# Layer 0's feed-forward: 14 of its 22 pairs of up tiles as seven block products in place of eight

## The chip, the cores and the metric

The kernel runs on one core of a Trainium2 chip. TensorE (PE) multiplies, VectorE (DVE) and ScalarE (ACT) do the elementwise work, GpSimd (POOL) a little of it, SyncE (SP) starts the transfers. Each engine works through its own list of instructions in the order written, and waits on semaphores for the others. The metric is the device time of one execution, in microseconds (us): the median of three runs of the kernel before is 1257.51, from 1257.15 to 1257.99.

## The reference

Two networks run one after the other on 256 tokens of width 1024. The first is one layer of gated linear attention with its feed-forward. The second has two layers and two streams: 256 latent tokens (the first network's output) and 256 context tokens. Layer 0 is neighbourhood attention, layer 1 grouped-query attention. Both streams are normalised, scaled and shifted by rows of an adaptive modulation that is computed from a conditioning vector. The stage that matters here is layer 0's feed-forward:

```python
def swiglu_ffn(h, w_in, w_out):
    a, g = jnp.split(h @ w_in, 2, axis=-1)
    return (jax.nn.silu(a) * g) @ w_out
...
        mod_l = (silu_c @ ada_w[i] + ada_b[i])[:, None, :]
        mod_c = (silu_cc @ ada_w[i] + ada_b[i])[None, None, :]
...
        h = h + g2_l * swiglu_ffn(ada_norm(h, norm_ffn[i], sh2_l, sc2_l), ffn_w_in[i], ffn_w_out[i])
        if ctx_out:
            hc = hc + g1_c * y_c
            hc = hc + g2_c * swiglu_ffn(ada_norm(hc, norm_ffn[i], sh2_c, sc2_c), ffn_w_in[i], ffn_w_out[i])
```

The width is 1024, the hidden width 2816: 22 tiles of 128 for `a` and 22 for `g`. A tile of `a` and the tile of `g` that is multiplied with it are called a pair. Layer 0 computes both streams, layer 1 only the latents' result.

## The kernel before

**Products.** Every 32-bit product is made of three matmuls (`mm3`, lines 192 to 195): each operand `x` is held as `h`, a rounded copy that PE multiplies fast, and `l = x - h`, and `h h + l h + h l` is summed in PSUM. So every weight that arrives has to be split first: ACT writes `h` (line 178), DVE subtracts (line 179). A weight unit is 128 x 1024 numbers (512 KB); `UNITS` lists all of them in the order of use, `wnext` hands out the next one, starts loads four ahead into five `raw` buffers, and splits ahead by a small number (`cap`).

**The feed-forward of layer 0.** Its tokens, 256 latents and 256 context tokens, lie transposed, split and side by side in `fT`, so a matmul moves 512 columns. It runs in two parts of 11 pairs. In the ups (`ffn_up`) each of the pair's two units is multiplied, 8 blocks of 128 times three matmuls, into a PSUM bank of 512; then `ffn_act` makes silu (ACT, line 1111), the product of the two banks (DVE, line 1112) and its split (lines 1118 and 1119). Behind a part's ups its down (`ffn_down0`) multiplies the 11 hidden tiles into four token tiles, one 512-wide half of the output at a time, and `gated` (lines 1080 and 1081) scales the sum by a modulation row and adds it to the residual. In the second part the context's tiles go first, so that the context can be normalised and transposed (`to_T`, lines 232 to 251) for layer 1 inside the latents' down (`between`); then the latents follow, and layer 1 begins with the context's and then the latents' key/value product.

**Modulation.** `ada_jobs` works through steps of one 512 KB load each (two buffers `a`) and one or two DVE reductions over 1024 elements (line 324). `adaC` holds 56 steps, spread over layer 0's feed-forward: two per pair in both parts and one per down unit of part one. A step for both streams has two reductions, one for the latents alone has one.

**Order.** A scheduler of the tile framework decides in which order instructions are given to each engine in this stage; what it decided stands in the program, and the engine follows it.

## Time and profile before

| | us |
|---|---|
| median of three runs | 1257.51 |
| profiled execution, its own time | 1256.72 |
| its span (first to last instruction) | 1254.9 |
| PE busy / DVE busy / ACT busy | 1244.0 / 919.9 / 688.2 |
| layer 0's feed-forward in the span | about 557 to 925 |
| DVE busy in it | 241.2 |

The mean granted TensorE clock is 0.999. Busy time counts from an instruction's start to its end; the next one of the same engine may start before that end, so the time that an instruction takes from its engine is the distance to the next start where nothing is waited for.

### The profile page before, as it was taken

How to read it: one execution, taken by the hardware profiler on the slowest of the kernel's cores; microseconds unless marked ns; L12 is line 12 of the kernel's file. 1: busy time of each engine (PE TensorE's matmuls, PEld its weight loads, DVE VectorE, ACT ScalarE, POOL GpSimd, SP SyncE). 2: the span in 40 equal slices, each digit the busy share in tenths (PEclk: the TensorE clock that was granted, in tenths of full speed). 3: DMA queues.
4: the chain of work that ended last, by engine and by line, in shares of the span. 5: the costliest groups of instructions: out<-in, count | busy, mean ns of one | idle time of the engine just before them, and what ended most of it. 6: DMA issues, size and time to landing. Idle time of an engine off the chain costs nothing.

```text
span 1254.9 us, 18667 instructions
## 1 busy us (share of the span) xinstructions
PE 1244.0 (99%) x6872; PEld 1043.2 (83%) x6872; DVE 919.9 (73%) x1638; ACT 688.2 (55%) x1344; POOL 78.7 (6%) x137
## 2 busy tenths in 40 slices
...
GB/s 304 189 151 237 192 289 268 271 277 246 198 249 111 105 110 118 160 197 118 213 177 206 259 266 249 205 100 102 197 204 76 113 84 131 219 187 185 186 185 34
DMA packets 68507, 231.22 MB, mean 184 GB/s; under 512 B 8048, under 2 KB 8736, under 8 KB 68416
## 3 DMA queue, kind: packets, MB, share of 16 engines
...
## 4 chain that ended last, share of the span: by engine, by line
PE 95%; ACT 2%; DVE 1%; issue 1%; DMA 0%; POOL 0%; SPq 0%; POOLq 0%; ACTq 0%
PE b L193 28%; PE b L194 28%; PE b L195 28%; PE b L1000 2%; PE b L1469 1%; PE b L981 1%; PE b L232 1%; PE b L1455 1%; PE b L562 1%; PE b L962 1%; PE b L963 1%; PE b L951 1%; PE b L1436 1%; DVE wl L179 0%; DMA t<-in_xt_dram 0%
## 5 line engine op out<-in xcount | busy, mean ns | idle before, releaser
L178 ACT CAST wh<-raw 128x1024 fp32r<-128x1024 f32 (+1 forms) x308 | 320.7, 1045 | 392.8 <-PE b L194 292.4
L179 DVE TENSOR_TENSOR wl<-raw,wh 128x1024 fp32r<-128x1024 f32 (+1 forms) x308 | 372.5, 1216 | 154.9 <-ACT wh L178 151.9
L193 PE MATMUL b<-t,wh 128*128 128x256 f32 (+1 forms) x1120 | 365.7, 327 | 0.0
L194 PE MATMUL b<-t,wl 128*128 128x256 f32 (+1 forms) x1120 | 365.6, 327 | 0.0
L195 PE MATMUL b<-t,wh 128*128 128x256 f32 (+1 forms) x1120 | 365.3, 327 | 0.0
L193 PE MATMUL b<-wh,t 128*128 128x512 f32 (+1 forms) x748 | 299.2, 402 | 1.2 <-ACT t L250 0.6
L194 PE MATMUL b<-wh,t 128*128 128x512 f32 (+1 forms) x748 | 294.8, 394 | 0.0
L195 PE MATMUL b<-wl,t 128*128 128x512 f32 (+1 forms) x748 | 294.7, 394 | 0.0
L193 PEld LDWEIGHTS b<-t,wh 128*128 128x128 f32 x1120 | 210.7, 188 | 22.2
L194 PEld LDWEIGHTS b<-t,wl 128*128 128x128 f32 x1120 | 210.8, 188 | 21.9
L195 PEld LDWEIGHTS b<-t,wh 128*128 128x128 f32 x1120 | 210.5, 188 | 20.4 <-DVE t L251 0.2
L195 PEld LDWEIGHTS b<-wl,t 128*128 128x128 f32 x748 | 140.4, 188 | 34.2
L193 PEld LDWEIGHTS b<-wh,t 128*128 128x128 f32 x748 | 140.4, 188 | 32.2 <-ACT t L250 1.0
L194 PEld LDWEIGHTS b<-wh,t 128*128 128x128 f32 x748 | 140.8, 188 | 30.1 <-DVE t L251 0.5
L324 DVE CUSTOM_DVE_ANT_0 a<-a,crow 128x1024 f32<-128x1024 f32 x96 | 117.6, 1233 | 28.8 <-DMA a<-in_ada_dram 28.3
L324 DVE CUSTOM_DVE_ANT_0 t<-a,crow 128x1024 bf16<-128x1024 f32 x64 | 78.5, 1237 | 7.3 <-DMA a<-in_ada_dram 7.1
L1112 DVE TENSOR_TENSOR t<-b,t 128x512 f32<-128x512 f32 (+1 forms) x42 | 23.7, 564 | 59.4 <-PE b L195 52.2
L205 POOL TENSOR_TENSOR c<-c,mhalf 128x1 f32<-128x1 f32 x21 | 14.2, 676 | 539.0 <-DVE c L204 538.9
L339 POOL TENSOR_TENSOR mod<-mod,bcol 128x8 f32<-128x8 f32 x20 | 13.4, 671 | 475.1 <-DVE mod L324 472.7
L1118 ACT CAST t<-t 128x512 fp32r<-128x512 f32 (+1 forms) x42 | 21.7, 516 | 28.6 <-DVE t L1112 28.6
L212 ACT ACTIVATE t<-t 128x512 f32<-128x512 f32 x40 | 24.8, 624 | 10.8 <-DVE t L1081 6.4
L1445 ACT ACTIVATE t<-b,c,c 128x512 f32<-128x512 f32 x32 | 26.0, 812 | 3.5 <-POOL c L1443 3.5
...
## 6 DMA issues: line engine op xcount, KB each, us to landing
raw<-in_wst_dram SPq DMA_DIRECT2D x310, 512.0 KB, 4.4
a<-in_ada_dram SPq DMA_DIRECT2D x96, 512.0 KB, 4.4
...
crow<-in_cvec_dram SPq DMA_DIRECT2D x2, 512.0 KB
```

The costliest lines, as they stand in the source:

```text
L178: A.copy(out=h[:, :n], in_=raw[:, :n])
L179: V.tensor_tensor(out=l[:, :n], in0=raw[:, :n], in1=h[:, :n], op=ALU.subtract)
L193: T.matmul(o, lhsT=lh, rhs=rh, start=first, stop=False)
L194: T.matmul(o, lhsT=ll, rhs=rh, start=False, stop=False)
L195: T.matmul(o, lhsT=lh, rhs=rl, start=False, stop=last)
L205: G.tensor_tensor(out=ms[:, 3:4], in0=ms[:, 2:3], in1=mhalf[:, 0:1], op=ALU.pow)
L212: A.activation(out=junk[hf], in_=halves[hf], func=AF.Square, scale=1.0 / 32.0, accum_out=ms[:, hf:hf + 1])
L324: V.tensor_tensor_reduce(out=raw if ci == n_c - 1 else t2([D], BF16), in0=raw, in1=crow[ci], scale=1.0, scalar=0.0, op0=ALU.mult, op1=ALU.add,
L1000: T.matmul(po[e * 64:(e + 1) * 64, cols_], lhsT=v, rhs=probs[(head, "l" if lat_q else "c")][:, c, :], start=(c == 0), stop=(c == n_c - 1))
L1112: V.tensor_tensor(out=a, in0=pg_[:, :n], in1=a, op=ALU.mult)
L1118: A.copy(out=h, in_=a)
L1445: A.activation(out=pl, in_=sl, func=AF.Exp, scale=r, bias=mx[:, 1:2], accum_out=mx[:, 2:3])
```

## The change

The first 8 pairs stay as they were, but their moving operand is cut into latents (`fL`) and context (`fC`), 256 columns each. The other 14 pairs are taken as a product of two-by-two blocks: the weights' two units (`a` and `g`) times the two halves of the width, and the two halves of the width times the two token streams. Seven products of blocks stand for the eight, each 4 blocks times three matmuls of 256 columns, with sums of weight blocks and of token blocks as operands (the form with four sums on each side and seven additions behind).

- `token_sums` makes the four sums of token blocks and their splits, in part one's down.
- `pair_sums` makes a pair's four sums of weight blocks (`z`, twice, `y`, `x`) and the splits: of `x`, `z` and `y` in full and of a half of 1024, three and a half in place of two.
- `ffn_up7` runs the seven products into three PSUM banks (`r`, `r23`, `r4`), ACT copies three of the intermediate sums out, and DVE combines: seven instructions of 256 columns, and the closing split of 512 with a change of sign.
- There are three parts, of 8, 8 and 6 pairs, in place of two of 11; so there is one more down with its four accumulators and its `gated` for each half, and every down unit is whole: 28 units in place of 36.
- `adaC` loses the 8 steps of (1, 5), which become `adaD`, called in layer 1's feed-forward; two steps per pair run in part one only, and the steps in the downs become one per unit in part one (first half), three and then one in part two, one in part three up to the last. The gates of (1, 5) are loaded in layer 1's feed-forward. `between` stands at the second of three units in place of the third of six.

```diff
-HALF = NFT // 2
+PARTS = ((0, 8), (8, 16), (16, 22))
+F_SEVEN = 8
...
-    for part in range(2):
-        for f in range(part * HALF, (part + 1) * HALF):
+    for lo, hi in PARTS:
+        for f in range(lo, hi):
             u += [("f", "ffn_in0", P * f), ("f", "ffn_in0", FH + P * f)]
-        dn = [("h", "ffn_out0", part * HALF + f, 512 * h) for h in range(2) for f in range(0, HALF, 2)]
-        u += dn if part == 0 else dn + dn
+        dn = [("h", "ffn_out0", f, 512 * h) for h in range(2) for f in range(lo, hi, 2)]
+        u += dn if hi < NFT else dn + dn
...
+    def seven(u):
+        return u[1] == "ffn_in0" and u[2] % FH >= P * F_SEVEN
...
-        while wpos[1] < len(UNITS) and wpos[1] - wpos[2] + 1 < cap[0]:
+        while wpos[1] < len(UNITS) and wpos[1] - wpos[2] + 1 < cap[0] and not seven(UNITS[wpos[1]]):
...
-    adaC = ada_jobs([(0, 5, True), (1, 0, True), (1, 1, True)] + [(1, v, False) for v in (3, 4, 2, 5)])
+    adaC = ada_jobs([(0, 5, True), (1, 0, True), (1, 1, True)] + [(1, v, False) for v in (3, 4, 2)])
+    adaD = ada_jobs([(1, 5, False)])
...
-    def ffn_up(L, src, n):
+    def ffn_up(L, src, n, conv=iter(())):
         ps_ = []
         for _ in range(2):
             u = wnext(("f", f"ffn_in{L}"))
             o = bank()
-            for k in range(KD):
-                mm_f(o[:, :n], u, src, k, 0, n, k == 0, k == KD - 1)
+            for t, X in enumerate(src):
+                for k in range(KD):
+                    mm_f(o[:, t * S:(t + 1) * S], u, X, k, 0, S, k == 0, k == KD - 1)
+            run(conv, 2)
             ps_.append(o)
...
+    def token_sums(j):
+        lo, hi, q = fX[j], fX[j + KD // 2], t2([2, S])
+        V.tensor_tensor(out=q[:, 1, :], in0=hi[:, 1, :], in1=lo[:, 1, :], op=ALU.subtract)
+        V.scalar_tensor_tensor(out=q[:, 0, :], in0=q[:, 1, :], scalar=-1.0, in1=lo[:, 0, :], op0=ALU.mult,
+                               op1=ALU.subtract)
+        V.tensor_tensor(out=lo[:, 1, :], in0=lo[:, 0, :], in1=lo[:, 1, :], op=ALU.subtract)
+        V.scalar_tensor_tensor(out=lo[:, 0, :], in0=q[:, 0, :], scalar=-1.0, in1=hi[:, 0, :], op0=ALU.mult,
+                               op1=ALU.subtract)
+        for z, names in ((q, (2, 1)), (lo, (4, 3))):
+            h, l = t2([2, S], F32R), t2([2, S], F32R)
+            A.copy(out=h, in_=z)
+            V.tensor_tensor(out=l, in0=z, in1=h, op=ALU.subtract)
+            for i, name in enumerate(names):
+                sT[(name, j)] = (h[:, i, :], l[:, i, :])
+    def pair_sums(f, got):
+        i = wpos[1]
+        assert UNITS[i] == ("f", "ffn_in0", P * f)
+        w_load(i + 4)
+        x, y = raws.pop(i), raws.pop(i + 1)
+        z = sb.tile([P, 1024], F32, tag="raw", bufs=5, name=nm("raw"))
+        wpos[1] += 2
+        a, b = slice(0, 512), slice(512, 1024)
+        def parts(r):
+            h = sb.tile([P, 1024], F32R, tag="w", bufs=NW, name=nm("wh"))
+            l = sb.tile([P, 1024], F32R, tag="w", bufs=NW, name=nm("wl"))
+            A.copy(out=h, in_=r)
+            V.tensor_tensor(out=l, in0=r, in1=h, op=ALU.subtract)
+            got.append((h, l))
+        parts(x)
+        yield
+        V.tensor_tensor(out=z[:, a], in0=x[:, a], in1=y[:, a], op=ALU.add)
+        V.tensor_tensor(out=z[:, b], in0=z[:, a], in1=y[:, b], op=ALU.add)
+        parts(z)
+        yield
+        V.tensor_tensor(out=y[:, a], in0=y[:, a], in1=y[:, b], op=ALU.add)
+        parts(y)
+        yield
+        V.tensor_tensor(out=x[:, a], in0=z[:, b], in1=x[:, b], op=ALU.add)
+        hl = sb.tile([P, 1024], F32R, tag="w", bufs=NW, name=nm("w"))
+        A.copy(out=hl[:, a], in_=x[:, a])
+        V.tensor_tensor(out=hl[:, b], in0=x[:, a], in1=hl[:, a], op=ALU.subtract)
+        got.append((hl[:, a], hl[:, b]))
+        yield
+    def splits(n):
+        for _ in range(n):
+            w_split(wpos[1] + 1)
+            yield
+    def ffn_up7(got, conv):
+        wpos[2] += 2
+        r, r23, r4 = bank(), bank(), bank()
+        c1, c2 = t2([2, S]), t2([2, S])
+        H = KD // 2
+        def prod(o, n, c, X, first=True):
+            h, l = got[n]
+            for j in range(H):
+                k = slice(c + j * P, c + (j + 1) * P)
+                mm3(o, h[:, k], l[:, k], *X(j), first and j == 0, j == H - 1, not first)
+        run(conv, 2)
+        prod(r[:, 0:S], 0, 0, lambda j: fL[j])
+        A.copy(out=c1[:, 0, :], in_=r[:, 0:S])
+        prod(r23[:, 0:S], 0, 512, lambda j: fL[H + j])
+        got[0] = None
+        V.tensor_tensor(out=c1[:, 0, :], in0=r23[:, 0:S], in1=c1[:, 0, :], op=ALU.add)
+        run(conv)
+        prod(r[:, 0:S], 1, 512, lambda j: sT[(2, j)], False)
+        A.copy(out=c1[:, 1, :], in_=r[:, 0:S])
+        A.activation(out=c1[:, 0, :], in_=c1[:, 0, :], func=AF.Silu)
+        prod(r23[:, S:N2], 2, 512, lambda j: sT[(4, j)])
+        run(conv)
+        prod(r[:, 0:S], 1, 0, lambda j: sT[(1, j)], False)
+        got[1] = None
+        A.copy(out=c2[:, 0, :], in_=r[:, 0:S])
+        V.tensor_tensor(out=c2[:, 1, :], in0=c1[:, 1, :], in1=c2[:, 0, :], op=ALU.subtract)
+        V.tensor_tensor(out=c2[:, 0, :], in0=r23[:, S:N2], in1=c2[:, 0, :], op=ALU.add)
+        V.tensor_tensor(out=c2[:, 0, :], in0=c2[:, 0, :], in1=c1[:, 0, :], op=ALU.mult)
+        prod(r4[:, 0:S], 3, 0, lambda j: fC[H + j])
+        V.tensor_tensor(out=c2[:, 1, :], in0=r4[:, 0:S], in1=c2[:, 1, :], op=ALU.add)
+        prod(r[:, 0:S], 2, 0, lambda j: sT[(3, j)], False)
+        V.tensor_tensor(out=c2[:, 1, :], in0=r[:, 0:S], in1=c2[:, 1, :], op=ALU.add)
+        A.activation(out=c2[:, 1, :], in_=c2[:, 1, :], func=AF.Silu)
+        V.tensor_tensor(out=c2[:, 1, :], in0=r[:, 0:S], in1=c2[:, 1, :], op=ALU.mult)
+        a = c2.rearrange("p t s -> p (t s)")
+        h, l = t2([N2], F32R), t2([N2], F32R)
+        A.activation(out=h, in_=a, func=AF.Copy, scale=-1.0)
+        V.scalar_tensor_tensor(out=l, in0=a, scalar=-1.0, in1=h, op0=ALU.mult, op1=ALU.subtract)
+        return h, l
...
+    def ffn_down0(hf, uu, tiles, n_ada, between=None, conv=None):
         ac = {t: bank() for t in tiles}
-        for f2 in range(0, HALF, 2):
+        for f2 in range(0, len(uu), 2):
             u = wnext(("h", "ffn_out0"))
-            for j in range(min(2, HALF - f2)):
+            for j in range(2):
                 f = f2 + j
                 for t in tiles:
-                    mm_h(ac[t], u, j, uu[f], t, f == 0, f == HALF - 1)
-            ada_run(adaC)
-            if f2 == 4 and between is not None:
+                    mm_h(ac[t], u, j, uu[f], t, f == 0, f == len(uu) - 1)
+            if n_ada:
+                ada_run(adaC, n_ada)
+            n = f2 // 2 - 2 + 4 * hf
+            if 0 <= n < 4 and len(sT) < 16:
+                token_sums(n)
+            if conv is not None and f2 >= len(uu) - 4:
+                run(conv, 2)
+            if f2 == 2 and between is not None:
                 between()
...
+    got = []
+    for lo, hi in PARTS:
         uu = []
-        for f in range(HALF):
-            if part == 0 and f < 2:
-                uu += ffn_up_first(fT) if f == 0 else []
+        for f in range(lo, hi):
+            nxt = []
+            if f + 1 < hi:
+                conv = pair_sums(f + 1, nxt) if f + 1 >= F_SEVEN else iter(())
             else:
-                uu.append(ffn_up(0, fT, N2))
-            ada_run(adaC, 2)
-        if part == 0:
+                conv = splits(2) if f >= F_SEVEN else iter(())
+            if f < 2:
+                uu += ffn_up_first() if f == 0 else []
+            elif f < F_SEVEN:
+                uu.append(ffn_up(0, (fL, fC), N2, conv))
+            else:
+                uu.append(ffn_up7(got, conv))
+            got = nxt
+            if lo == 0:
+                ada_run(adaC, 2)
+        if lo == 0:
             load_gates(0, 5)
-            for hf in range(2):
-                ffn_down0(hf, uu, (2, 3, 0, 1))
+        if hi < NFT:
+            ffn_down0(0, uu, (2, 3, 0, 1), 3 if lo else 1)
+            got = []
+            ffn_down0(1, uu, (2, 3, 0, 1), 1 if lo else 0, None, pair_sums(hi, got) if hi >= F_SEVEN else None)
         else:
             for hf in range(2):
-                ffn_down0(hf, uu, (2, 3))
+                ffn_down0(hf, uu, (2, 3), 1)
             xn = [normed(t) for t in hc]
-            ffn_down0(0, uu, (0, 1))
+            ffn_down0(0, uu, (0, 1), 1)
             bT2 = new_T2()
             ada_run(adaC, 100)
             cap[0] = 7
-            ffn_down0(1, uu, (0, 1), lambda: to_T(xn, bT2, S, mod(1, 1, 1), mod(1, 1, 0)))
+            ffn_down0(1, uu, (0, 1), 0, lambda: to_T(xn, bT2, S, mod(1, 1, 1), mod(1, 1, 0)))
...
+        if f < 12:
+            ada_run(adaD)
+        if f == 12:
+            load_gates(1, 5)
```

The order that the scheduler made of it changes at three places that matter.

PE in the ups. The rows name the bank on the left, then the moving and the standing operand (`t` tokens, `wh` and `wl` the two parts of a weight). Before, in the ups of part two, all matmuls of a unit stand together:

```order
L195 MATMUL b_6780<-t_5765,wh_6685 128x512
L193 MATMUL b_6780<-t_5766,wh_6685 128x512
L194 MATMUL b_6780<-t_5766,wl_6686 128x512
L195 MATMUL b_6780<-t_5767,wh_6685 128x512
L193 MATMUL b_6811<-t_5752,wh_6716 128x512
L194 MATMUL b_6811<-t_5752,wl_6717 128x512
L195 MATMUL b_6811<-t_5753,wh_6716 128x512
L193 MATMUL b_6811<-t_5754,wh_6716 128x512
```

Now, in the first pair of part three: `b_8949` is the bank `r` of pair 16, `b_9074` a bank of pair 17; all are 256 columns wide.

```order
L199 MATMUL b_8949<-t_7488,wl_8894 128x256
L200 MATMUL b_8949<-t_7489,wh_8893 128x256
L200 MATMUL b_9074<-t_5753,wh_8955 128x256
L198 MATMUL b_9074<-t_5754,wh_8955 128x256
L199 MATMUL b_9074<-t_5754,wl_8956 128x256
L200 MATMUL b_9074<-t_5754,wh_8955 128x256
L198 MATMUL b_8949<-t_7342,wh_8929 128x256
L199 MATMUL b_8949<-t_7342,wl_8930 128x256
L200 MATMUL b_8949<-t_7343,wh_8929 128x256
```

The next pair's first product is drawn in between the products of this one, as soon as its first split can be there.

DVE behind the down that precedes the last ups. Rows of line 1080 (1086 now) read the down's accumulators, those of line 1081 (1087) add to the residual, `ISA` with `a` is a reduction of a modulation step, with `mod` alone its read-out. Before, behind part one's down:

```order
L1081 TENSOR_TENSOR t_80<-t_7593,t_80 128x512
L324 ISA a_7815,mod_7560<-a_7815,crow_87 128x1024
L324 ISA mod_7560 128x1
L179 TENSOR_TENSOR wl_7749<-raw_7627,wh_7748 128x1024
L324 ISA a_7818,mod_7892<-a_7818,crow_87 128x1024
L324 ISA mod_7892 128x1
L341 SCALAR_TENSOR_TENSOR mod_7560<-mod_7560,sm 128x8
L324 ISA a_7890,mod_7892<-a_7890,crow_87 128x1024
L324 ISA mod_7892 128x1
L1112 TENSOR_TENSOR t_7658<-b_7633,t_7658 128x512
L179 TENSOR_TENSOR wl_7780<-raw_7671,wh_7779 128x1024
```

Now, behind part two's down, up to the first combination (line 1239) of pair 16:

```order
L1087 TENSOR_TENSOR t_5737<-t_8940,t_5737 128x512
L1086 TENSOR_TENSOR t_8943<-b_8787,t_7214 128x512
L1086 TENSOR_TENSOR t_8946<-b_8788,t_7214 128x512
L329 ISA a_8767,mod_8686<-a_8767,crow_87 128x1024
L329 ISA mod_8686 128x1
L1087 TENSOR_TENSOR t_78<-t_8943,t_78 128x512
L329 ISA a_8770,mod_8821<-a_8770,crow_87 128x1024
L329 ISA mod_8821 128x1
L1087 TENSOR_TENSOR t_80<-t_8946,t_80 128x512
L1203 TENSOR_TENSOR raw_8954<-raw_8824,raw_8857 128x512
L1239 TENSOR_TENSOR t_8952<-b_8950,t_8952 128x256
```

The reductions stand among the additions and ahead of the weight sums (line 1203) and the combination; in the rows from the first of these additions to pair 20's first combination there are 12 of them, 14 splits of 1024, 37 instructions of 512 and 28 of 256.

DVE at the junction to layer 1, where the context's transposed tiles are scaled, shifted and split (lines 248 and 251 before, 253 and 256 now). Before:

```order
L251 TENSOR_TENSOR t_8786<-t_8884,t_8785 128x256
L251 TENSOR_TENSOR t_8788<-t_8891,t_8787 128x256
L248 TENSOR_SCALAR t_8898<-b_8895,mod_7006,mod_6674 128x256
L251 TENSOR_TENSOR t_8790<-t_8898,t_8789 128x256
L179 TENSOR_TENSOR wl_8940<-raw_8827,wh_8939 128x1024
L251 TENSOR_TENSOR t_8792<-t_8905,t_8791 128x256
L248 TENSOR_SCALAR t_8912<-b_8909,mod_7006,mod_6674 128x256
L179 TENSOR_TENSOR wl_8958<-raw_8845,wh_8957 128x1024
L251 TENSOR_TENSOR t_8794<-t_8912,t_8793 128x256
L179 TENSOR_TENSOR wl_8976<-raw_8863,wh_8975 128x1024
L251 TENSOR_TENSOR t_8796<-t_8919,t_8795 128x256
L248 TENSOR_SCALAR t_8926<-b_8923,mod_7006,mod_6674 128x256
```

Now:

```order
L253 TENSOR_SCALAR t_10038<-b_10035,mod_7259,mod_6810 128x256
L329 ISA a_11904,mod_11908<-a_11904,crow_87 128x1024
L329 ISA mod_11908 128x1
L256 TENSOR_TENSOR t_9944<-t_10038,t_9943 128x256
L329 ISA a_11906,mod_11908<-a_11906,crow_87 128x1024
L329 ISA mod_11908 128x1
L180 TENSOR_TENSOR wl_10094<-raw_9993,wh_10093 128x1024
L256 TENSOR_TENSOR t_9946<-t_10045,t_9945 128x256
L253 TENSOR_SCALAR t_10052<-b_10049,mod_7259,mod_6810 128x256
L256 TENSOR_TENSOR t_9948<-t_10052,t_9947 128x256
L256 TENSOR_TENSOR t_9950<-t_10059,t_9949 128x256
L253 TENSOR_SCALAR t_10066<-b_10063,mod_7259,mod_6810 128x256
```

Reductions of (1, 5), emitted in layer 1's feed-forward, stand between these rows: five here, and two more between the latents' gated additions and their normalisation, where there was none. From part two's down to the latents' first split there are 26 reductions, 32 splits of 1024, 63 instructions of 512 and 58 of 256.

38 lines of the change are left out of this document (18 added, 20 removed).

## The prediction

> **What bounds the kernel now.** I read the page's engine table and chain of waits first.
>
> ```profile
> span 1254.9 us, 18667 instructions
> PE 1244.0 (99%) x6872; PEld 1043.2 (83%) x6872; DVE 919.9 (73%) x1638; ACT 688.2 (55%) x1344; POOL 78.7 (6%) x137
> PE 95%; ACT 2%; DVE 1%; issue 1%; DMA 0%; POOL 0%; SPq 0%; POOLq 0%; ACTq 0%
> ```
>
> TensorE (PE) is never really waiting, and 95% of the chain that ended last is its own. Fewer PE cycles shorten the kernel as long as nobody makes PE wait. So I cut the layer-0 feed-forward out of the trace as windows: its ups of part one, its first down with the start of part two, and the rest; then the whole, and the junction to layer 1.
>
> ```profile
> 557.00:670.00 113.00, 113.00 (x585) 95.16 (x584) 88.40 (x140) 42.25 (x68) 6.92 (x18) 1.00 0.55 170
> 670.00:790.00 120.00, 120.00 (x515) 96.53 (x514) 86.27 (x129) 27.55 (x32) 3.76 (x5) 1.00 0.77 251
> 790.00:925.00 135.00, 135.00 (x582) 108.42 (x581) 66.53 (x80) 46.29 (x61) 2.20 (x3) 1.00 0.50 154
> 557.00:925.00 368.00, 368.00 (x1679) 300.11 (x1678) 241.20 (x348) 116.09 (x161) 12.88 (x26) 1.00 0.60 191
> 925.00:1000.00 75.00, 74.37 (x384) 59.34 (x382) 62.56 (x136) 55.87 (x136) 17.19 (x28) 1.00 0.40 120
> ```
>
> Columns after the stretch: its length, then busy PE, weight loads, VectorE (DVE), ScalarE (ACT), POOL, granted clock, DMA share, GB/s. PE is busy for all 368 us; DVE for 241.2, so 127 us of DVE are free. But the free time lies late (66.5 of 135 busy) and the change adds DVE work in every later pair. That is the question of this case: PE work is traded for DVE work, on an engine that runs its queue strictly in the order it was given.
>
> **What PE saves.** How long a matmul holds PE is the distance of starts, not the duration.
>
> ```profile
> 599.73 0.40 PE L195 MATMUL b<-t,wh 128*128 128x512 f32 x1
> ...
> 605.82 0.40 PE L194 MATMUL b<-t,wl 128*128 128x512 f32 x1
> ...
> 1099.53 0.28 PE L195 MATMUL b<-t,wh 128*128 128x256 f32 x1
> ...
> 1100.93 0.28 PE L195 MATMUL b<-t,wh 128*128 128x256 f32 x1
> ```
>
> The first two are the first and the last of 27 rows, 6.09 / 26 = 0.234 us apart at 512 columns; the others of 13, 1.40 / 12 = 0.117 us at 256: half. So cutting the moving operand of the first eight pairs into latents and context costs nothing. A pair was 48 matmuls of 512 = 11.2 us; a pair by seven products is 7 x 4 x 3 = 84 of 256 = 9.8 us, twelve fewer than 96. 14 pairs x 12 x 0.117 = **-19.7 us**. The down products keep their number of matmuls. [...]
>
> **What DVE gets.** These groups give durations, the timeline rows the distance of starts when DVE is not held.
>
> ```profile
> L179 DVE TENSOR_TENSOR wl<-raw,wh 128x1024 fp32r<-128x1024 f32 x302 | 368.4, 1227 | 154.9 <-ACT wh L178 151.9 <-DMA raw<-in_wst_dram 0.8
> L324 DVE CUSTOM_DVE_ANT_0 a<-a,crow 128x1024 f32<-128x1024 f32 x96 | 117.6, 1233 | 28.8 <-DMA a<-in_ada_dram 28.3
> L1112 DVE TENSOR_TENSOR t<-b,t 128x512 f32<-128x512 f32 x22 | 15.2, 690 | 42.9 <-PE b L195 35.7 <-PE b L348 6.5 <-ACT t L1111 0.7
> L1112 DVE TENSOR_TENSOR t<-b,t 128x256 f32<-128x256 f32 x20 | 8.5, 425 | 16.5 <-PE b L195 16.5
> ...
> 584.26 1.23 DVE L179 TENSOR_TENSOR wl<-raw,wh 128x1024 fp32r<-128x1024 f32 x1 [0.20 <-ACT wh L178]
> 585.41 0.68 DVE L1119 TENSOR_TENSOR t<-t,t 128x512 fp32r<-128x512 f32 x1
> 586.01 1.22 DVE L324 CUSTOM_DVE_ANT_0 t<-a,crow 128x1024 bf16<-128x1024 f32 x1
> ...
> 572.99 1.42 DVE L251 TENSOR_TENSOR t<-t,t 128x256 fp32r<-128x256 f32 x4
> 574.68 0.42 DVE L251 TENSOR_TENSOR t<-t,t 128x256 fp32r<-128x256 f32 x1 [0.27 <-ACT t L250]
> ```
>
> Back to back a 1024-element instruction takes 1.15 us, a 512 one 0.60, a 256 one (1.42 - 0.42) / 3 = 0.333, with 0.335 taken; their durations are 1.23, 0.69 and 0.42. A pair before: two splits and two 512 instructions, 2 x 1.15 + 2 x 0.60 = 3.5 us beside 11.2 of PE. A pair by seven: three full splits, a half split, four weight sums, the closing split of 512, seven combinations of 256: 3 x 1.15 + 6 x 0.60 + 7 x 0.335 = **9.4 us** beside 9.8 (10.8 by durations). DVE is now as loaded as PE before anything else stands in its queue.
>
> Part two's ups: between the first combination of pair 8 and the closing split of pair 15 stand 27 instructions of 1024, 43 of 512, 56 of 256: 31.1 + 25.8 + 18.8 = 75.6 us against 8 x 9.83 = 78.6 of PE. The eight gated additions of the extra part (8 x 0.60 = 4.8) come just ahead. Lower bound 0; upper bound by durations 86.2 + 5.5 - 78.6 = 13 us. The rows show instructions that don't need each other at their distances, and that gives 80.4 - 78.6 = 1.8, from which weight sums done ahead in the down go off: I take **+1**, with 3 as the forecast's own upper end.
>
> Part three and the junction. Here the order decides. Behind the gated additions that wait for the last matmul of part two's down stand reductions of the modulation steps (L329; L324 before), which before ran beside lightly loaded pairs. From there to pair 20's first combination (L1239) the queue holds 12 reductions, 14 splits of 1024, 37 of 512, 28 of 256: 26 x 1.15 + 37 x 0.60 + 28 x 0.335 = 61.5 us. PE has some 400 matmuls of 256 ahead of the one that needs that value (four pairs, three products of the fifth, and what of the sixth the order has drawn ahead): 46.8 us. The additions begin ahead of PE's first product, since the first of the four accumulators is complete nine matmuls of 512 before the last (2.1 us; I take 1.8). DVE is late by 61.5 - 46.8 - 1.8 = 12.9 us, while six pairs save only 6 x 1.4 = 8.4. Further on, to the instruction that frees PE's first latent key/value product of layer 1 (L256, L251 before), the whole is 58 of 1024 (26 of them reductions), 63 of 512, 58 of 256 and a few of one column: 66.7 + 37.8 + 19.4 + 0.5 = 124.4 us, less 1.8 = 122.6. PE's own work to the same place: 6 x 9.83 = 59.0, four downs of 36 x 0.234 = 33.7, the context's key/value product 48 x 0.234 = 11.2, transposes some 1.5: 105.4. The two differ by **+17.2 us**. This takes in the 12.9, it does not come on top.
>
> Seven of these 26 reductions are steps of (1, 5), emitted in layer 1's feed-forward; the order has them in the junction, five among the context's transposes, two inside the latents' norm. In the trace of before that place looks so:
>
> ```profile
> 938.25 1.28 DVE L1080 TENSOR_TENSOR t<-b,t 128x512 f32<-128x512 f32 x2
> 939.45 1.28 DVE L1081 TENSOR_TENSOR t<-t,t 128x512 f32<-128x512 f32 x2
> ...
> 945.01 1.00 DVE L248 TENSOR_SCALAR t<-b,mod,mod 128x256 f32<-128x256 f32 x2 [0.79 <-PE b L232]
> 946.12 1.10 DVE L251 TENSOR_TENSOR t<-t,t 128x256 fp32r<-128x256 f32 x3
> PE b L193 <- ACT t L250: 0.6, 1, 0.6
> ```
>
> From the down's end to the first split latents pass 7.9 us, of which DVE's own instructions fill about 5; PE, fed with the context's product, waited 0.6 us. So this chain was covered with nothing to spare, and what DVE is late there PE is late too. The chain's waits for ACT, POOL and PE, and DVE's waits for ACT's copies ahead of each split, add **+2** (1, since the reductions fill some; up to 5, two thirds of a us in each of six pairs beside it).
>
> Reductions also wait for their loads:
>
> ```profile
> 706.16 1.23 DVE L324 CUSTOM_DVE_ANT_0 a<-a,crow 128x1024 f32<-128x1024 f32 x1 [1.84 <-DMA a<-in_ada_dram]
> 707.63 1.22 DVE L324 CUSTOM_DVE_ANT_0 a<-a,crow 128x1024 f32<-128x1024 f32 x1 [0.23 <-DMA a<-in_ada_dram]
> 711.84 1.23 DVE L324 CUSTOM_DVE_ANT_0 a<-a,crow 128x1024 f32<-128x1024 f32 x1 [1.84 <-DMA a<-in_ada_dram]
> a<-in_ada_dram SPq DMA_DIRECT2D x96, 512.0 KB, 4.4
> ```
>
> Two buffers, 4.4 us a landing: two steps per 5.7 us. The first eight reductions of part three stand 17 us apart in all and need 7 x 2.85 = 20; the last four of the junction some 2 us closer than that. **+3.5** (0 if loads run ahead, 6 if each pair waits as above).
>
> ```profile
> L178 ACT CAST wh<-raw 128x1024 fp32r<-128x1024 f32 x302 | 317.0, 1054 | 382.0 <-PE b L194 285.7 <-issue 74.3 <-DMA a<-in_ada_dram 9.1
> L1118 ACT CAST t<-t 128x512 fp32r<-128x512 f32 x22 | 13.7, 621 | 25.7 <-DVE t L1112 25.7
> ```
>
> What costs nothing, and its cover: ACT's work per seven-pair, three full casts and seven instructions of 512 or 256 (half a cast, three copies, two silu, the closing cast), is 3 x 1.05 + 7 x 0.62 = 7.5 us of 9.8 even with all seven at 512's price; the tokens' sums, 16 x 0.335 + 8 x 0.60 = 10.2 us of DVE, lie in part one's down, where PE has 45 us and DVE was busy 86 of 120; the eight loads and splits fewer are gain only where DVE binds, in neither down. The moved loads of (1, 5) pass through SP's queue ahead of weights, at a DMA share of 0.40 in that stretch.
>
> **The sum.** -19.7 + 1 + 17.2 + 2 + 3.5 = **+4.0 us** on the profiled run: span 1254.9 + 4.0, plus the 1.8 around it (the run was 1256.72), plus 0.8 by which the median 1257.51 stands above: 1261.5, said as 1261. Its bounds: 0, 17.2, 1 and 0 give -1.5; 3, 17.2, 5 and 6 give +11.5: 1256 to 1269.
>
> [...]
>
> **Rivals.**
> *DVE keeps up (1243, 0.12).* On the average over the stage it does: 241 + 14 x 5.9 + 10 + 10 = 344 us beside 348 of PE. Then only part two's 1 us and some 4 of the junction are lost: 1257.5 - 19.7 + 5. Against: the reductions stand behind the gated additions, so they can't use earlier idle time.
> *The junction hides it (1251.5, 0.13).* DVE makes up its lag in part three's four downs, and only the 12.9 stay: -19.7 + 1 + 12.9 = -5.8. It decides if the late reductions give way to the context's product. Against: 124.4 us are in the queue whatever their places.
> *Later still (1272, 0.18).* Instructions depend on each other and take durations. That would be 139.7 us for 124.4; if most are held so, +11 on the sum.
> *The clock falls (1266, 0.05).*
>
> ```profile
> 1245.00:1250.00 5.00, 2.98 (x25) 2.78 (x23) 4.75 (x13) 2.86 (x8) 0.54 (x1) 1.00 0.16 60
> 1250.00:1254.90 4.90, 0.00 (x0) 0.00 (x0) 0.54 (x2) 0.72 (x1) 0.55 (x1) 0.81 0.41 153
> ```
>
> After PE's last matmul, the granted clock is 1.00 for 2 us and then 0.81 over 4.9. If the lag becomes four gaps of some 5 us, each followed by 5 us of work at 0.81, each costs 5 x (1/0.81 - 1) = 1.2 us, together +5. Against: 22 us of lag over some 42 products and four downs make short gaps. [...]
>
> **How the numbers follow.** The forecast holds 0.52, around 1261, its own range 1256 to 1269. A measurement tells 0.2% (2.5 us) from no change. Faster (below 1255.0): 0.12 and 0.09 of the second rival, 0.21. Same (1255.0 to 1260.0): 0.04 of it and 0.20 of the forecast, 0.24. Slower: 0.32 of the forecast, 0.18 and 0.05, together 0.55. The range 1249 to 1271 leaves out the first rival and a part of the third.
>
> **What would show it.** PE rows in the ups: a seven-pair of 9.8 us where it isn't held. Groups of PE waits: little in pairs 8 to 15; DVE (L1198, L1213, L1239, L256) and ACT behind it as releasers from pair 16 to the junction, in all 15 to 28 us. A DVE busy to nine tenths there. Reductions (L329) between the gated additions and L1239, some with idle time put down to their load. Granted clock 1.00 throughout. I'm wrong if PE's idle time in part three stays under 8 us, or if it lies in pairs 8 to 15.

## The result, and the profile after

The changed kernel takes 1273.21 us at the median of four runs (1272.06 to 1274.17), against 1257.51 before: a ratio of 1.0124, with a 95% interval of 1.0108 to 1.0140. It is slower by 15.7 us, where +4.0 on the profiled execution was forecast. The two profiled executions, on which the rest of this text goes, differ by the same: spans of 1270.3 and 1254.9 us, +15.4.

The engine table and the chain of waits of the page after:

```profile
span 1270.3 us, 20549 instructions
PE 1238.2 (97%) x7664; PEld 1073.8 (85%) x7664; DVE 1013.7 (80%) x1838; ACT 724.6 (57%) x1428; POOL 80.5 (6%) x137
PE 79%; DVE 10%; DMA 4%; ACT 2%; issue 2%; POOL 0%; SPq 0%; POOLq 0%; ACTq 0%; DVEq 0%
```

PE's share of the chain that ended last fell from 95% to 79%; DVE has 10% of it and the loads of the modulation steps 4%. PE's work became less and PE now waits. Where, the windows tell. In the changed kernel the three stretches hold most of part two's ups, part three, and the junction to layer 1; before, with its two parts of 11 pairs, the same times hold other pieces of the stage. Columns after the stretch: its length, busy PE, weight loads, DVE, ACT, POOL, granted clock, DMA share, GB/s. First before:

```profile
700.00:785.00 85.00, 85.00 (x365) 68.35 (x364) 61.12 (x92) 18.93 (x21) 3.22 (x5) 1.00 0.78 258
836.00:910.00 74.00, 74.00 (x320) 59.35 (x319) 35.63 (x43) 28.12 (x39) 1.08 (x2) 1.00 0.47 141
910.00:970.00 60.00, 60.00 (x285) 48.64 (x284) 43.90 (x88) 36.27 (x79) 9.33 (x12) 1.00 0.47 142
```

and after:

```profile
700.00:785.00 85.00, 82.30 (x640) 78.50 (x639) 74.21 (x121) 44.76 (x74) 0.00 (x0) 1.00 0.38 118
836.00:910.00 74.00, 64.31 (x465) 59.95 (x466) 70.89 (x120) 36.74 (x58) 0.58 (x1) 0.95 0.65 219
910.00:970.00 60.00, 53.21 (x235) 41.60 (x234) 52.94 (x96) 31.28 (x66) 7.23 (x10) 0.94 0.58 188
```

In the stretch of part three DVE went from 35.63 us busy of 74 to 70.89, and PE idles for 9.7 us there and 6.8 in the junction. The granted clock, 1.00 in every stretch of before, is 0.95 and 0.94. The forecast's sum took 1.00 throughout. Two places of PE's timeline show where it comes from (start, duration, and in brackets the idle time ahead with its releaser):

```profile
840.50 0.28 PE L200 MATMUL b<-t,wh 128*128 128x256 f32 x1
845.53 0.58 PE L198 MATMUL b<-t,w 128*128 128x256 f32 x1 [4.75 <-ACT w L1212]
...
847.47 0.41 PE L200 MATMUL b<-t,w 128*128 128x256 f32 x1
847.69 0.41 PE L198 MATMUL b<-t,w 128*128 128x256 f32 x1
...
849.61 0.44 PE L199 MATMUL b<-t,wl 128*128 128x256 f32 x1
849.89 0.28 PE L200 MATMUL b<-t,wh 128*128 128x256 f32 x1
850.01 0.28 PE L198 MATMUL b<-t,wh 128*128 128x256 f32 x1
...
938.03 0.44 PE L237 MATMUL b<-cm,t 128*128 128x128 f32 x2 [1.41 <-ACT t L250]
940.35 0.77 PE L198 MATMUL b<-wh,t 128*128 128x512 f32 x1 [1.89 <-DVE t L253]
940.92 0.63 PE L199 MATMUL b<-wh,t 128*128 128x512 f32 x1
941.34 0.63 PE L200 MATMUL b<-wl,t 128*128 128x512 f32 x1
...
945.51 0.40 PE L198 MATMUL b<-wh,t 128*128 128x512 f32 x1
```

Between 840.50 and 845.53, in pair 16, PE was idle for 4.75 us. After that matmuls of 256 start 0.21 to 0.22 us apart, where 0.117 was the distance of before, until 849.61; then 0.12 again. In the junction it was idle twice, 1.41 and 1.89 us, with only two transposes between, and for 5 us the products of 512 start 0.42 apart instead of 0.234. The 4.1 us of the one stretch lose about 4.1 x (1 - 0.117 / 0.213) = 1.8 us, the 5 of the other 5 x (1 - 0.234 / 0.427) = 2.2: an estimated **4.0 us** of PE's time. Whether the kernel is longer by them is another question, taken up further down.

Why PE stood in pair 16, the queues of DVE and ACT tell:

```profile
825.27 1.28 DVE L1086 TENSOR_TENSOR t<-b,t 128x512 f32<-128x512 f32 x2
826.47 1.22 DVE L329 CUSTOM_DVE_ANT_0 a<-a,crow 128x1024 f32<-128x1024 f32 x1
...
834.16 1.23 DVE L329 CUSTOM_DVE_ANT_0 a<-a,crow 128x1024 f32<-128x1024 f32 x1 [0.63 <-DMA a<-in_ada_dram]
...
836.52 0.42 DVE L1239 TENSOR_TENSOR t<-b,t 128x256 f32<-128x256 f32 x1
...
839.51 1.23 DVE L329 CUSTOM_DVE_ANT_0 a<-a,crow 128x1024 f32<-128x1024 f32 x1 [0.23 <-DMA a<-in_ada_dram]
...
842.93 1.22 DVE L329 CUSTOM_DVE_ANT_0 a<-a,crow 128x1024 f32<-128x1024 f32 x1
...
844.08 0.69 DVE L1210 TENSOR_TENSOR raw<-raw,raw 128x512 f32<-128x512 f32 x1
...
844.86 0.62 ACT L1212 CAST w<-raw 128x512 fp32r<-128x512 f32 x1 [4.48 <-DVE raw L1210]
...
888.33 0.41 DVE L1239 TENSOR_TENSOR t<-b,t 128x256 f32<-128x256 f32 x1
...
959.21 1.77 DVE L256 TENSOR_TENSOR t<-t,t 128x256 fp32r<-128x256 f32 x5
```

Reductions (L329) stand between the gated additions that wait for part two's last product and pair 16's first combination (L1239), and again ahead of the last weight sum (L1210). ACT's cast of that sum (L1212) waits 4.48 us for it, and PE's product waits for the cast. That is the place and the kind that the forecast named.

### The profile page after: what moved, and what is told of

Same layout as the page of the kernel before. It is cut to its first block, busy times and chain, and to the rows that moved or that the text cites. A ratio compares the mean times of both kernels' runs of the same rounds, so it can differ in the third digit from the quotient of the medians.

```text
span 1270.3 us, 20549 instructions
## 1 busy us (share of the span) xinstructions
PE 1238.2 (97%) x7664; PEld 1073.8 (85%) x7664; DVE 1013.7 (80%) x1838; ACT 724.6 (57%) x1428; POOL 80.5 (6%) x137
## 4 chain that ended last, share of the span: by engine, by line
PE 79%; DVE 10%; DMA 4%; ACT 2%; issue 2%; POOL 0%; SPq 0%; POOLq 0%; ACTq 0%; DVEq 0%
PE b L198 23%; PE b L199 22%; PE b L200 22%; DMA a<-in_ada_dram 4%; DVE wl L1198 2%; PE b L1006 2%; DVE a L329 1%; PE b L1602 1%; PE b L987 1%; DVE wl L180 1%; PE b L1588 1%; ACT wh L179 1%; PE b L237 1%; PE b L568 1%; PE b L968 1%
## 5 line engine op out<-in xcount | busy, mean ns | idle before, releaser
L180 DVE TENSOR_TENSOR wl<-raw,wh 128x1024 fp32r<-128x1024 f32 x272 | 331.5, 1229 | 126.0 <-ACT wh L179 125.2
L179 ACT CAST wh<-raw 128x1024 fp32r<-128x1024 f32 x272 | 284.8, 1053 | 248.6 <-PE b L199 199.8
L198 PE MATMUL b<-t,wh 128*128 128x256 f32 (+1 forms) x1328 | 388.4, 294 | 5.5 <-DVE t L1239 3.0
L199 PE MATMUL b<-t,wl 128*128 128x256 f32 (+1 forms) x1328 | 386.9, 292 | 0.0
L200 PE MATMUL b<-t,wh 128*128 128x256 f32 (+1 forms) x1328 | 386.3, 292 | 0.0
L198 PEld LDWEIGHTS b<-t,wh 128*128 128x128 f32 x1328 | 249.6, 188 | 17.8 <-DVE t L1239 3.4
L199 PEld LDWEIGHTS b<-t,wl 128*128 128x128 f32 x1328 | 250.2, 188 | 7.6
L200 PEld LDWEIGHTS b<-t,wh 128*128 128x128 f32 x1328 | 249.8, 188 | 5.8 <-DVE t L256 0.2
L329 DVE CUSTOM_DVE_ANT_0 a<-a,crow 128x1024 f32<-128x1024 f32 x96 | 117.7, 1233 | 7.3 <-DMA a<-in_ada_dram 7.0
L329 DVE CUSTOM_DVE_ANT_0 t<-a,crow 128x1024 bf16<-128x1024 f32 x64 | 78.2, 1229 | 10.8 <-DMA a<-in_ada_dram 10.6
L1197 ACT CAST wh<-raw 128x1024 fp32r<-128x1024 f32 x42 | 43.9, 1050 | 25.7 <-PE b L199 12.3
L1198 DVE TENSOR_TENSOR wl<-raw,wh 128x1024 fp32r<-128x1024 f32 x42 | 51.1, 1223 | 2.9 <-ACT wh L1197 1.5
L1119 DVE TENSOR_TENSOR t<-b,t 128x256 f32<-128x256 f32 (+1 forms) x28 | 14.0, 501 | 27.8 <-PE b L200 23.6
```

The lines of the kernel that those rows point to most:

```text
L179: A.copy(out=h[:, :n], in_=raw[:, :n])
L180: V.tensor_tensor(out=l[:, :n], in0=raw[:, :n], in1=h[:, :n], op=ALU.subtract)
L198: T.matmul(o, lhsT=lh, rhs=rh, start=first, stop=False, skip_group_check=onto)
L199: T.matmul(o, lhsT=ll, rhs=rh, start=False, stop=False, skip_group_check=onto)
L200: T.matmul(o, lhsT=lh, rhs=rl, start=False, stop=last, skip_group_check=onto)
L329: V.tensor_tensor_reduce(out=raw if ci == n_c - 1 else t2([D], BF16), in0=raw, in1=crow[ci], scale=1.0, scalar=0.0, op0=ALU.mult, op1=ALU.add,
```

## The experiments

Two theories at first. **The queue:** DVE's in-order queue, with the reductions standing in it, holds PE; the 15 us are a matter of what stands ahead of what. **The loads:** the reductions' loads, two buffers deep, pace DVE and crowd the weights. Later a third: that the steps are bunched in the wrong part. Every run is compared with the kernel before on the same chip.

### The reductions' time, without their loads being touched

From the 21st modulation step on, the reductions run over 8 of 1024 columns; the loads stay. The sums of those steps, and what follows from them, are not computed.

```diff
+                w_ = D if n < thin else 8
-                V.tensor_tensor_reduce(out=raw ..., in0=raw, in1=crow[ci], ...
+                V.tensor_tensor_reduce(out=raw[:, 0:w_] ..., in0=raw[:, 0:w_], in1=crow[ci][:, 0:w_], ...
```

> The changed kernel with the modulation reductions from the 21st step of the list on (all of parts two and three and the junction) taken over 8 of 1024 columns; loads and order of steps stay. Left out are the sums over the other 1016 columns. Theory QUEUE (the reductions' own DVE time, 1.15 us each, in part three's queue and in the junction is what PE waits for): some 25 us come back, about 1248, PE's idle time left only in pairs 8 to 15. Rival LOADS (the pace of the two load buffers, 2.8 us a step, is what DVE's queue moves at): little comes back, 1266 to 1270, since the loads are as before. Rival WORK (the sums and combinations of a seven-pair alone overload DVE, wherever reductions stand): 1262 to 1266.

Measured 1254.14 us, a ratio of 0.9970 (0.9959 to 0.9980): 19 us less than the change. So without the reductions' time on DVE the 15 us are gone. But it is also only 3.3 us faster than before, of some 18 that PE saves, and 6 us slower than the queue theory's number. By the sum over PE's starts that is explained further down, its profiled execution loses 4.9 us in part two's ups and 4.7 in part three, and 6.4 more than before from 900 to 985, at the junction: so the seven-product pairs and the junction use up most of the gain with hardly a reduction beside them.

### The loads, left out

Those steps' loads are left out instead and the reductions sum the tile at hand at full length; again these sums are not the reference's.

```diff
-                nc.sync.dma_start(out=loaded[n], in_=ada[(L * 6 + v) * KD + k])
+                if n < thin:
+                    nc.sync.dma_start(out=loaded[n], in_=ada[(L * 6 + v) * KD + k])
...
-                V.tensor_tensor_reduce(out=raw if ci == n_c - 1 else t2([D], BF16), in0=raw, ...
+                V.tensor_tensor_reduce(out=raw if ci == n_c - 1 else t2([D], BF16), in0=raw if n < thin else crow[1 - ci], ...
```

> The changed kernel with the loads of the same modulation steps left out; the reductions run in full over a tile that is already there, so those modulation rows are not computed from their weights. QUEUE: only the waits for loads come back, 1267 to 1270. LOADS: most comes back, about 1250. WORK: 1268 to 1272.

Measured 1256.11 us, 0.9992 (0.9982 to 1.0002), with the reductions' full time on DVE: 11 us below the queue theory's range and 6 above what the loads theory said. The windows, columns as above:

```profile
700.00:785.00 85.00, 80.79 (x626) 76.58 (x625) 84.61 (x143) 42.61 (x70) 1.71 (x2) 1.00 0.34 110
836.00:910.00 74.00, 71.69 (x519) 66.39 (x518) 69.85 (x117) 38.78 (x62) 0.40 (x2) 1.00 0.42 137
```

DVE is busy for 84.61 of 85 us in part two's ups, against 74.21 in the change: the order has 13 of these reductions in that stretch, where the change has none, and none from 910 to 970, where the change has ten. Eight of the 13 stand one in each pair, five behind the last pair's first combination. PE's waits are many and short there, and the clock stays at 1.00. So the same DVE work can be queued at a cost of some 17 us less. Whether the missing loads do that themselves or by the order that they allow isn't told apart by this run.

### The loads, three buffers deep

```diff
-                loaded[n] = sb.tile([P, D], F32, tag="ada", bufs=2, name=nm("a"))
+                loaded[n] = sb.tile([P, D], F32, tag="ada", bufs=3, name=nm("a"))
```

(The room is taken from the pool of temporaries, 56 for 58.)

> The changed kernel with three buffers for the modulation steps' loads in place of two (two of the 58 working tiles given for it). Nothing else is changed in the code; the scheduler may place reductions earlier. After two runs, LOADS now says: the pace of the loads (two steps per 5.7 us) pushes the reductions of part two's down behind the down's gated additions, and in its place DVE sits idle earlier; with three buffers 8 to 14 us come back, 1259 to 1265. QUEUE, by which the number of reductions in the stage counts and not when their loads land: 1270 to 1273.

One group of reductions (count, busy us, mean ns, idle time ahead and what ended it), whose idle time put down to loads was 10.6 us in the change:

```profile
L329 DVE CUSTOM_DVE_ANT_0 t<-a,crow 128x1024 bf16<-128x1024 f32 x64 | 77.8, 1226 | 1.0 <-DMA a<-in_ada_dram 1.0
```

and what PE waited for longest (us in total, times, longest):

```profile
PE b L199 <- DVE w L1213: 7.3, 1, 7.3
```

Together with the other group (7.0 us in the change) the waits fell from 17.6 to 5.3. The time: 1273.77, 1.0130 (1.0115 to 1.0145), that of the change. DVE's stalls on landings aren't what costs; it loses the time at the half split instead. This takes pacing out of the loads theory.

### The loads, issued and not read

To have the loads' traffic without anyone waiting for it, the reductions sum the tile at hand, as in the second experiment, beside loads that are issued; in the same steps the sums are not the reference's.

```diff
-                V.tensor_tensor_reduce(out=raw if ci == n_c - 1 else t2([D], BF16), in0=raw, ...
+                V.tensor_tensor_reduce(out=raw if ci == n_c - 1 and n < thin else t2([D], BF16), in0=raw if n < thin else crow[1 - ci], ...
```

> Left out: from the 21st modulation step on, the reductions sum the tile at hand instead of the newly loaded one, as in e2_noload, but the loads are issued (their data go unread), so the sums and what follows from them are not the reference's. The order of the reductions differs from the change's: none stands in the part of pairs 8 to 15's ups, 20 stand in part two's down work, 12 in the down work of part three, none among part three's ups. Theory A, the queue on VectorE by prefixes: no reduction stands ahead of a pair's sums in the seven-product pairs, so the time is as e2_noload, 1252 to 1259. Theory B, the traffic of the loads itself (16 queues' transfers beside the weights, or the stalls of VectorE on their landing) is what makes e2_noload 17 us shorter than the change: then the traffic back makes it 1264 to 1274. Between the two (1259 to 1264) both have a share.

Measured 1275.01 us, 1.0132 (1.0115 to 1.0149). That is 1 us above the range of the traffic theory, but it doesn't decide. What PE waited for longest, a DVE group of part two's ups, and a window there:

```profile
PE b L353 <- POOL mod L344: 14.7, 1, 14.7
```

```profile
L1203 DVE TENSOR_TENSOR raw<-raw,raw 128x512 f32<-128x512 f32 x6 | 4.1, 689 | 6.5 <-DMA raw<-in_wst_dram 6.5
```

```profile
720.00:760.00 40.00, 33.96 (x274) 32.47 (x273) 33.48 (x56) 20.00 (x33) 0.00 (x0) 1.00 0.80 280
```

The loads now run ahead in SP's queue in one bunch, the DMA share is 0.80 in part two's ups, the weights of the block sums come late (6.5 us), and 12 reductions end up in the junction, where PE's small transpose of their sums (L353) waits 14.7 us for the last of them, and PE's queue with it. Both are new. It shows what loads in front of weights can cost, and that no reduction among a pair's sums is no cure by itself; the question that it was made for stays open, as the order changed with it.

### Other places for the reductions

The steps of (1, 5) loaded through the weights' buffers, so that they can't run ahead and stay in layer 1's feed-forward:

```diff
-    def ada_jobs(jobs):
+    def ada_jobs(jobs, ring=("ada", 2)):
...
-    adaD = ada_jobs([(1, 5, False)])
+    adaD = ada_jobs([(1, 5, False)], ("raw", 5))
```

> The changed kernel with the eight steps of (1,5) loaded into the weights' buffers, so that the scheduler leaves them in layer 1's feed-forward; the order up to the junction is the same row for row. QUEUE: seven reductions of 1.15 us and their load waits leave the junction, and with them the second low-clock stretch: 1261 to 1265. LOADS: about 3 us of waits, 1269 to 1271. WORK: 1272 or more, nothing comes back.

Measured 1267.26 us, 1.0077 (1.0062 to 1.0092): the junction's reductions cost 6 us of the 15.7, 2 less than the least that the queue theory forecast.

The spread of the steps as before (two in each pair of all parts, one per unit of the downs, (1, 5) in the list):

```diff
...
-            if lo == 0:
-                ada_run(adaC, 2)
+            ada_run(adaC, 2)
...
-            ffn_down0(0, uu, (2, 3, 0, 1), 3 if lo else 1)
+            ffn_down0(0, uu, (2, 3, 0, 1), 1)
```

> The changed kernel with the old spread of the modulation steps: two per pair in all three parts, one per down unit, the eight of (1,5) in the same list; no step in the junction. The order has 2 reductions per pair in pairs 8 to 13, ten around the end of part two, seven in its down, three in part three. QUEUE by row sums: a pair of part two is 9.4 + 2.3 = 11.7 us of DVE against 9.83, 8 x 1.9 + 2 = 17 us late in part two; part three and the junction keep up, and cost 2 to 4: -19.7 + 17 + 3 + 3 = about 1261, 1257 to 1264. LOADS: evenly spread loads cost no waits, 1250 to 1254.

Measured 1271.26, 1.0106 (1.0087 to 1.0126). That is 7 us above the queue theory's range. The reductions are gone from the junction, and the loss has moved to part two: PE's longest waits, and two windows.

```profile
PE b L198 <- DVE t L1086: 4.2, 1, 4.2
PE b L199 <- DVE wl L1198: 3.5, 1, 3.5
```

```profile
700.00:720.00 20.00, 13.98 (x94) 12.96 (x92) 19.61 (x34) 4.73 (x9) 1.32 (x2) 0.83 0.40 123
720.00:740.00 20.00, 17.25 (x124) 17.25 (x125) 20.00 (x35) 9.95 (x17) 0.00 (x0) 0.83 0.48 156
```

One gap of 4.2 us that ends at 706.88 and one of 3.5 that ends at 722.75, and a granted clock of 0.83 in the window of each. Then the opposite of the change: hardly a reduction in part three and none in the junction, three steps a pair in pairs 10 to 15, one per unit in the first half of each of the downs, the steps of (1, 5) late as two runs above.

```diff
             if lo == 0:
                 ada_run(adaC, 2)
+            elif 10 <= f < 16:
+                ada_run(adaC, 3)
...
```

> All 14 pairs by seven products; the modulation steps moved out of part three and the junction: three per pair in pairs 10 to 15, one per unit in the first half of part two's down, (1,5) loaded through the weights' buffers and left in layer 1's feed-forward. The order then has no reduction from part three's first combination to the key/value product, and 22 among the combinations of pairs 10 to 15. QUEUE by prefixes (DVE late wherever its row sum runs ahead of PE's): part two 75.6 + 4.8 + 22 x 1.15 = 105.7 against 78.6, part three and the junction 1 to 4: -19.7 + 20 to 27 + 3 + 1, 1262 to 1268. Rival BUNCH (what costs is only a group of reductions between a down's gated additions and the first combination, and a spread reduction is absorbed): 1250 to 1254.

Measured 1269.77, 1.0101 (1.0086 to 1.0116). Three places for the reductions, and 1270 to 1273 each time, so the bunch in the change isn't the only cause: these orders move PE's waits and don't take them away. With 14 pairs in sevens and the loads in place, no order that was tried has room for them. One was not tried: one reduction in each pair of part two, as the run without loads has it; these runs had two and three.

### Fewer pairs in sevens

Which of the 14 pay? Six early ones (8 to 13), and six late ones (16 to 21), everything else as in the change; for the early ones:

```diff
-        return u[1] == "ffn_in0" and u[2] % FH >= P * F_SEVEN
+        return u[1] == "ffn_in0" and P * F_SEVEN <= u[2] % FH < P * 14
```

(with the same bound where the sums are made; for the late ones F_SEVEN is 16 and there is no upper bound).

> Seven products for pairs 8 to 13 alone, eight for pairs 14 to 21 (moving operand 256 wide there too); parts and modulation steps as in the change. PE saves 6 x 12 x 0.117 = 8.4 us. QUEUE: part three's pairs have 3.5 us of DVE each again and take the reductions; only the six pairs' own waits of 3 to 5 us remain: 1251 to 1255. WORK: each seven-pair loses what it gains, 1257 or more. LOADS: reductions still paced by loads ahead of part three, 1258 to 1262.

> Seven products for pairs 16 to 21 alone: as many as in the run with pairs 8 to 13 (1256.6), but in part three, where the spilled reductions stand. PE saves 8.4 us. The order keeps the reductions among part three's pairs and in the junction. QUEUE and LOADS alike: part three's 14 to 16 us and the junction's 10 to 11 come whole, 1257.5 - 8.4 + 25 = 1274, 1270 to 1277. WORK (a seven-pair costs the same wherever it stands): 1255 to 1258.

Six early: 1256.61 us, 0.9996 (0.9987 to 1.0006). Six late: 1272.17, 1.0121 (1.0106 to 1.0136), on the span +14.3. The same number of products saved, and 15.6 us between them. But the early six too give back most of their 8 us: they are 0.8 us faster than before on the same chip, between what the queue theory (1251 to 1255) and its rival (1257 or more) said. Part three of the six early ones:

```profile
836.00:910.00 74.00, 74.00 (x561) 70.99 (x561) 53.27 (x75) 22.73 (x27) 2.43 (x3) 1.00 0.76 244
```

and part three and the junction of the six late ones:

```profile
836.00:910.00 74.00, 69.71 (x509) 65.19 (x508) 66.96 (x110) 35.21 (x58) 0.58 (x1) 0.98 0.60 196
910.00:970.00 60.00, 53.02 (x239) 41.17 (x238) 54.45 (x100) 31.77 (x67) 6.74 (x10) 0.94 0.56 190
```

```profile
741.76 0.28 PE L198 MATMUL b<-t,wh 128*128 128x256 f32 x1
...
747.93 0.28 PE L199 MATMUL b<-t,wl 128*128 128x256 f32 x1
```

This is the pair of runs that places what the change loses against before: in the last six pairs, whose sums stand behind part two's gated additions together with the reductions, and which nothing plain follows in which DVE could catch up. The last two rows, of the timeline of the six late ones, are the first and the last of 53 in pairs that nobody holds: 6.17 / 52 = 0.1187 us a matmul of 256, not 0.117.

### Versions

From the six early ones, with parts of 8, 6 and 8 pairs instead of 8, 8 and 6:

```diff
-PARTS = ((0, 8), (8, 16), (16, 22))
+PARTS = ((0, 8), (8, 14), (14, 22))
```

> Sevens for pairs 8 to 13 alone, with parts of 8, 6 and 8 pairs in place of 8, 8 and 6: part three's downs have four units, so two units of the latents' last down (5.6 us) stand behind the context's transposes in place of one. If the junction's extra 3 us of the run with pairs 8 to 13 come from that cover, they come back: 1253 to 1255. If they come from the reductions' order or from the end of the stage: 1256 to 1257.

1255.86, 0.9991 (0.9981 to 1.0000). Then the (1, 5) steps back in the list, ahead of layer 1:

> The kernel with parts of 8, 6 and 8 pairs and sevens for pairs 8 to 13 (1255.9), with (1,5) back in the one list of modulation steps and its gates loaded before layer 1's feed-forward, as before the change. All traces of kernels with the moved steps lose 0.7 to 1.0 us between layer 1's attention and its last gated addition. If the moved steps or gates cost that, it comes back: 1254.5 to 1255.3. If not: 1255.6 to 1256.2.

1256.14, 0.9991 (0.9982 to 1.0001): no difference. On top of that, one of a pair's block sums on POOL:

```diff
-V.tensor_tensor(out=y[:, a], in0=y[:, a], in1=y[:, b], op=ALU.add)
+G.tensor_tensor(out=y[:, a], in0=y[:, a], in1=y[:, b], op=ALU.add)
```

> As the run with the steps back, and the sum of a pair's second unit (512 elements, 0.60 us of DVE per pair) on POOL. No row shows a POOL addition of 512; the nearest, 128x256 at 1.45 us, gives 2.9 us for it. QUEUE: 0.6 us per pair off DVE in six pairs, 1 to 3 us less if POOL's longer time is hidden behind the other splits: 1252 to 1254. If the split that needs the sum comes too late: 1256 to 1262.

1259.75, 1.0019 (1.0009 to 1.0029): 3.6 us slower. The group, and PE's longest wait:

```profile
L1206 POOL TENSOR_TENSOR raw<-raw 128x512 f32<-128x512 f32 x6 | 15.3, 2545 | 68.4 <-DVE raw L1202 48.9 <-issue 10.0 <-ACT t L1242 9.4
PE b L198 <- DVE t L1238: 2.4, 1, 2.4
```

The sum lasts 2.5 us on POOL, where on DVE it lasts 0.69. But PE doesn't lose its time beside the later sums: the one long wait, 2.4 us, is for pair 8's first combination (line 1238 in this version), behind the gated additions, and matmuls start 0.21 apart for some 3.5 us after it. That POOL made this gap longer is likely and not shown. The version that it is made from has the same gap in its profiled execution, which at 1259.88 is the slowest of its ten:

```profile
706.00:712.00 6.00, 5.04 (x29) 5.04 (x30) 5.12 (x8) 3.30 (x5) 0.00 (x0) 0.72 0.37 113
```

PE was idle for 1.89 us just before 706.96 there, and the granted clock of this window is 0.72; the median of that version is 3.7 us less. And last, instead of POOL, pair 8 left plain, so that sevens begin one pair behind the gated additions of part two:

```diff
-F_SEVEN = 8
+F_SEVEN = 9
```

> As the run with the steps back, but pair 8, the first behind part one's down, by eight products; sevens for pairs 9 to 13. PE saves 7.0 instead of 8.4. QUEUE by prefixes: the loss of pairs 8 to 13 (3.7 us) is the first combinations standing behind eight gated additions; with a plain pair there DVE has 11.2 - 3.5 us to get clear, and 0 to 1 is lost: 1.5 to 2 us faster than the run with the steps back, 1252.5 to 1254. If the loss is per seven-pair, 0.6 each, the time stays or rises by up to 1.

1254.59, 0.9982 (0.9971 to 0.9992). It does 1.4 us less in sevens than the version that it is made from and is 1.55 faster: by the medians five pairs of seven give more than six, though the two intervals overlap. The same with parts of 8, 8 and 6 and sevens in pairs 9 to 14:

> As the change, but pairs 9 to 14 alone are of seven products (6 in place of 14), with parts of 8, 8 and 6 pairs as before and the step of (1,5) back in the list ahead of layer 1. The count by prefixes: six pairs save 6 x 1.4 = 8.4 us of TensorE time; pair 8 plain lets VectorE run off its eight gated additions first, so part two's ups give back 1 to 3, and the last part stays as before. Theory A: 1250 to 1255. If the last plain pair of part two does not let VectorE catch up ahead of part three, it is as m14_six_early, 1255 to 1258.

1255.82, 0.9984 (0.9975 to 0.9993): 0.8 us above the range of the first expectation, and inside that of the second. These two are the versions that are faster than before beyond the interval, if barely: by 0.18% (0.08 to 0.29) and 0.16% (0.07 to 0.25).

## Why the prediction was wrong

The direction was forecast at 0.55, and most of the place and the kind of the waits were right. The size was not, 4.0 against 15.4 us. The steps that failed are part two's ups, the waits inside DVE's queue in part three and the junction, and two terms put at nothing. PE's loss below is added up from its timeline: how much each distance of starts exceeds that of a matmul that nothing holds (0.118 us at 256 columns, 0.234 at 512). That is more than the idle time of the windows, since it counts the slower clock and gaps that a matmul's own duration (0.28 us at 256 columns) covers.

**What PE saves, -19.7.** Taken at 0.117 us a matmul from before's rows; those of the changed part start 0.118 apart on the mean, 0.1187 in the quiet rows above. 14 x (96 x 0.117 - 84 x 0.118) = 18.5, so 1.2 less. A small error: half the columns cost slightly more than half.

**Part two's ups, +1: measured 5.4.** A step that failed. I compared totals, 75.6 us of DVE with 78.6 of PE, and took what was over. But DVE is behind from the start: the last splits of the token sums (L1180), which I had put at nothing, stand ahead of the eight gated additions, and these ahead of pair 8's first combination, for which PE waits 1.42 us.

```profile
697.55 0.70 DVE L1180 TENSOR_TENSOR t<-t,t 128x512 fp32r<-128x512 f32 x1
698.15 1.30 DVE L1086 TENSOR_TENSOR t<-b,t 128x512 f32<-128x512 f32 x2
...
704.08 0.44 DVE L1239 TENSOR_TENSOR t<-b,t 128x256 f32<-128x256 f32 x1
...
704.57 0.39 PE L198 MATMUL b<-t,wh 128*128 128x256 f32 x1 [1.42 <-DVE t L1239]
```

So a comparison of totals misses the lag that DVE has on the way: PE's time lost early doesn't come back in the last pairs, where DVE in its turn waits. The gap at pair 8 is less than a third of the 5.4, though; one of 0.9 us follows at 736.50, and the rest is small pieces. Leaving pair 8 plain takes the gap at pair 8 away: that version's window of this stretch has PE busy for 84.47 of 85 us.

```profile
700.00:785.00 85.00, 84.47 (x595) 78.08 (x595) 68.06 (x111) 36.87 (x57) 1.32 (x2) 1.00 0.41 132
```

It doesn't take the whole loss away. By the same sum over starts this execution, the fastest of its eight, still loses 2.2 us with five pairs of seven; the other version with pair 8 plain loses 4.0 with six (the slowest of its ten), and the six early pairs, with pair 8 by seven products and no gap there, 3.2. What sets these smaller losses stays open.

**Part three and the junction, 17.2 + 2 + 3.5 = 22.7: measured 26.5.** The counting by the queue was right, the waits in it were not. From the gated additions at 825.27 to pair 20's first combination at 888.33 stand 63.1 us, for 61.5 counted and some load waits. To the first freeing instruction of the latents (L256, 959.21) it is 133.9. The window of just that stretch, and what DVE waited for in it (us in total, times, longest):

```profile
825.27:959.21 133.94, 117.52 (x731) 102.94 (x729) 124.41 (x211) 60.76 (x106) 5.32 (x7) 0.95 0.67 220
DVE a L329 <- DMA a<-in_ada_dram: 5.3, 6, 1.8
DVE t L224 <- POOL c L210: 1.5, 3, 0.7
DVE wl L180 <- ACT wh L179: 1.5, 2, 1.3
DVE t L256 <- ACT t L255: 0.9, 2, 0.5
```

DVE is busy for 124.4 us, as counted, and idle for 9.5, where I had added 2 + 3.5 = 5.5. This is the step that failed here: the waits inside the queue, 4.0 us too small. The 1.8 us by which the additions were to begin ahead of PE's first product were 0.2 (825.27 and 825.49), and PE's own work was longer by about as much. The six late pairs alone give the term nearly by itself: +14.3 on the span plus the 7.9 that they save, 22.2 us, the end's share in it. DVE's distances were as priced, 1.2 us for two of 512 and 1.14 for a reduction; "later still", which needed durations in their place and gave 1272, came to the time by another way, so its nearness is luck.

**The clock, given 0.05 and +5 us.** "Granted clock 1.00 throughout" was wrong: 0.95 and 0.94, an estimated 4.0 us of PE's time. I wrote that a lag of 22 us over 42 products makes short gaps. But in a queue that runs in order a lag is taken at the product whose operand is late, here once at 4.75 us and once in two gaps close together. That the rival's +5 is near is luck: it counted four gaps and a clock of 0.81, and there were two stretches at 0.55 of the rate. And the 4.0 us are not a term of the sum. In the rows just above DVE hardly waits for PE (under 0.1 us in the trace); only the 1.5 us behind ACT's weight casts can go back to it, since ACT there waited for PE to free buffers (5.5 us in five waits). DVE set the pace, and a faster PE would have stood longer for it. Where DVE has room a dip can cost: the two executions under Versions with a gap and a dip at pair 8 are 3.6 and 3.7 us above the median without, for gap and dip together, and in the one with POOL DVE waits for PE behind the dip, twice for 1.2 us.

That short gaps leave the clock at 1.00 was an estimate of mine, and the traces show it for some only. The clock came down behind the gap of 4.75 us here and behind those of 4.2 and 3.5 us with the old spread of the steps, where matmuls of 256 start 0.21 us apart behind each. But behind the junction's two gaps, of 1.41 and 1.89 us and two transposes apart, it came down too (0.42 us between starts of 512), and so it did behind the single one of 1.89 us under Versions (0.72 in the window).

**The loads, +3.5.** The waits are there, 17.6 us in all the kernel and 5.3 in the stretch above, but with three buffers they went to 5.3 in all the kernel and the time stayed. So the 9.5 us above are an account of one trace; it does not follow that shorter waits for loads alone give the time back.

**What was taken at nothing.** Besides the token sums: from layer 1's start on the lag of 13.5 us grows to 14.4 by its last gated addition, and the end adds 1.0. Together: -18.5 + 5.4 + 26.5 + 1.9 = +15.3, where 15.4 were measured.

**The signs that I named.** A seven-pair of 9.8 us where it isn't held: 84 x 0.118 = 9.9. PE's excess from pair 16 to the junction between 15 and 28 us: 26.5. "Little in pairs 8 to 15" was wrong and is a missing term; "granted clock 1.00 throughout" was wrong too, at no cost that the trace shows.

**What stays open.** Why the version without loads gets the same reductions done 17 us cheaper. Its order is better, its clock stays at 1.00 in the four stretches from 700 to 970, and it has no loads in SP's queue. Buffers (unchanged time) and places (1267 to 1273) were tried one at a time; its order with the loads in place was not. The queue theory is also short in its numbers: of the runs with all 14 pairs in sevens and the sums intact, all four came out above its range, by 0.8 to 7.3 us. So that DVE's queue holds PE is shown; how much of the 15.7 us the loads cause by the order that they force is not.
